# Two weight blocks split ahead of the first sums, the rest behind them, in a two-layer decoder trunk on one core

## The chip, the core and the metric

The kernel runs on one core of one Trainium2 chip. The metric is the device time of one execution in microseconds. The engines are named as in the profile: PE (matrix multiply), DVE (vector), ACT (scalar), POOL (GpSimd) and SP (which issues most loads from memory).

## The reference

The reference is a trunk of two layers with fp32 inputs. A layer is a half-step SwiGLU, a token mixer, and another half-step SwiGLU; a final RMS norm follows. With 256 tokens, width 1024 and 2816 hidden columns, the part that matters here is

```
def swiglu(x, w_gate, w_up, w_down):
    return (jax.nn.silu(x @ w_gate) * (x @ w_up)) @ w_down

x = x + 0.5 * swiglu(rms_norm(x, norm_ffn1[l]), w_ffn1_gate[l], w_ffn1_up[l], w_ffn1_down[l])
x = x + hybrid_mixer(rms_norm(x, norm_mix[l]), w_in[l], ...)
x = x + 0.5 * swiglu(rms_norm(x, norm_ffn2[l]), w_ffn2_gate[l], w_ffn2_up[l], w_ffn2_down[l])
```

So there are six phases in a row: SwiGLU, mixer, SwiGLU, SwiGLU, mixer, SwiGLU. The kernel numbers them `pi` 0 to 5.

## The kernel before

**Precision.** Every fp32 weight block of 128x1024 is split into a high part `whi` (ACT casts the raw block `wraw`, L260) and a low part `wlo` (DVE subtracts, L290). The same is done to the activations (`xh`, `xl`, side by side in `x2`). A product is made of three terms: high by high, high by low, low by high.

**Stream.** One `Stream` object carries all weight blocks in the order of their use. `loads` issues the transfers on SP into 5 buffers `wraw`. `split` issues the ACT cast of the next block and then the DVE subtraction of the block before it, which it had kept in `waiting`; `low` issues a subtraction that is still kept. The subtraction frees the block's `wraw` buffer, and the next load follows. There are 7 pairs of buffers for `whi` and `wlo`; `done` gives a pair back when PE has used it. `split` stops when none is free.

**SwiGLU phase.** The 2816 hidden columns are 22 groups of 128, numbered `j`. Group `j` needs a gate block and an up block; below they are called G0, U0, G1, U1, G2, and so on, and D0, D1 are the blocks of the down projection. `wide` multiplies one block in 8 steps; each step is a matmul of 512 columns with `whi` (L594) and one of 256 columns with `wlo` (L596). The two results of an even group go into two PSUM banks called psB, those of an odd group into psC and psD; each of these banks is single, so a group needs the banks of the group two before it to be read out. `read(j)` does that: per block ACT copies one half of the bank into the tile `hs` (L680) and DVE adds the other half to it (L681). These are the sums that the change speaks of. `finish(j)` then scales (POOL L691), applies SiLU (ACT L692), scales again (POOL L693), multiplies gate by up (DVE L695) and splits the product into `hp` (ACT L696, DVE L698), which the down matmuls (L572 to L574) take in.

**Start of a phase.** In the phases with `pi` > 0 the first two groups are multiplied by `gu_two`: first one half of the inner dimension for all four blocks, then `late()` turns the second half of the activations (`x_turn`, ACT L388 and DVE L389), then the second half of the inner dimension for all four. Then come `read(0)`, `read(1)` and the next round with the groups 2 and 3.

**What sets the order.** The program is written as one sequence; a scheduler with a timing model of its own then fixes the order of instructions on each engine, and on the chip every engine takes its instructions in that order. The kernel steers it with `st.behind`: what `split` and `low` put on ACT or DVE is queued behind the instruction named there (`queue`, L226). `x_turn` sets both entries to its last parts; `read(0)` sets the DVE entry to its last sum (L683). The phases 2, 3 and 5 are those with `gu_two` and `read` in this form; the mixers set `behind` by themselves.

Of the kernel before, what the change touches and what calls it, by code (L numbers as in the profile page):

```python
# [29 lines left out]
D, S, L, DH = 1024, 256, 2, 64  # L30
# [51 lines left out]
def all_units(phases):  # L82
    return [u for ph, l in phases for u in phase_units(ph, l)]
# [234 lines left out]
def trunk(ctx, tc, xin, wst, w1st, gains, glast, cst, small, out, phases=PHASES, n_raw=5, n_hl=7):  # L318
    nc = tc.nc
    V, A, G, T = nc.vector, nc.scalar, nc.gpsimd, nc.tensor  # L320
# [7 lines left out]
    st = Stream(nc, wst, all_units(phases), rawp, hlp, n_raw, n_hl)  # L328
# [3 lines left out]
    def load_aside(dst, src):  # L332

        with tc.issue_after(st.last):
            nc.sync.dma_start(dst, src)
# [3 lines left out]
    def bank(tag):  # L339
        return ps.tile([128, 512], F32, name="ps" + tag, tag="ps" + tag, bufs=BUFS[tag])  # L340
# [54 lines left out]
    def half_of(h):  # L395
        return slice(h * 512, (h + 1) * 512)
# [192 lines left out]
    def wide(o, u, ks):  # L589

        hi, lo = u[1]
        for k in ks:
            x = state["x2"][:, k]
            T.matmul(o, blk128(hi, k), x.rearrange("p a t -> p (a t)"), start=k == 0, stop=k == KT - 1,  # L594
                     skip_group_check=True)
            last = T.matmul(o[:, S:], blk128(lo, k), x[:, 0], start=False, stop=k == KT - 1,  # L596
                            skip_group_check=True).ins
        return last

    def wide_apart(o, u):  # L600

        hi, lo = u[1]
        for k in range(KT):
            T.matmul(o, blk128(hi, k), state["x2"][:, k].rearrange("p a t -> p (a t)"), start=k == 0, stop=k == KT - 1,
                     skip_group_check=True)
        for k in range(KT):
            T.matmul(o[:, S:], blk128(lo, k), state["x2"][:, k, 0], start=False, stop=k == KT - 1,
                     skip_group_check=True)

    def first_pair(os, us):  # L610

        xh, xl = state["xh"], state["xl"]
        for i, (o, u) in enumerate(zip(os, us)):
            hi, lo = u[1]
            for n in range(KT + 2 * LAG):
                if i == 0 and 0 < n < KT:
                    with tc.issue_after(real):
                        T.matmul(idle[:, :256], zero[:, :128], zero, start=True, stop=True)
                for p, (w, x, c) in enumerate(((hi, xh, 0), (hi, xl, S), (lo, xh, S))):
                    k = n - p * LAG  # L620
                    if 0 <= k < KT:
                        real = T.matmul(o[:, c:c + S], blk128(w, k), x[:, k], start=p == k == 0,
                                        stop=p != 1 and k == KT - 1, skip_group_check=True).ins
            st.done(u[0])
# [19 lines left out]
    def ffn(pi, name, l):  # L644
        nxt = pi + 1
        gu_tags = ["BB", "CD"]
        pend, S_ = {}, {}
        H = {}

        def gu_open(j):  # L650
            b = pend[j] = [bank(t) for t in gu_tags[j % 2]]
            return b, [st.use(what, name, l, j) for what in ("gate", "up")]

        def gu(j, mid=None):
            b, us = gu_open(j)
            if j == 0 and pi == 0:
                first_pair(b, us)
                return
            for o, u in zip(b, us):
                if j == 1 and pi == 0:  # L660
                    wide_apart(o, u)
                else:
                    wide(o, u, range(KT))
                st.done(u[0])
                if mid:
                    mid = mid()

        def gu_two():

            work = []  # L670
            for j in range(2):
                b, us = gu_open(j)
                work += [(lambda ks, o=o, u=u: wide(o, u, ks), [u]) for o, u in zip(b, us)]
            two_halves(work)

        def read(j):

            s = S_[j] = mp.tile([128, 2, S], F32, name="hs", tag="PT", bufs=5)
            for i, o in enumerate(pend.pop(j)):
                A.copy(s[:, i], o[:, S:])  # L680
                add = V.tensor_add(s[:, i], s[:, i], o[:, :S]).ins  # L681
            if j == 0 and pi > 0:
                st.behind["V"] = add  # L683

        def finish(j):
            n = 0 if j == NJ - 1 else 1
            s = S_.pop(j)
            g, u = s[:, 0], s[:, 1]
            hp = mp.tile([128, 2, S], F32R, name="hp", tag="qs", bufs=6)
            hh, hl = hp[:, 0], hp[:, 1]  # L690
            G.tensor_mul(g, g, state["rbc"])  # L691
            A.activation(g, g, AF.Silu)  # L692
            G.tensor_mul(g, g, state["rbc5"])  # L693
            st.split(n)
            V.tensor_mul(g, g, u)  # L695
            A.copy(hh, g)  # L696
            st.split(n)
            V.tensor_sub(hl, g, hh.bitcast(F32))  # L698
            st.split(3 - 2 * n)
            H[j] = hp  # L700

        def evac(j):
            read(j)
            finish(j)

        acc = {}
        last = nxt == len(phases)

        def down(j, u, t, h):
            if j == 0:  # L710
                acc[t, h] = bank("A")
            hi, lo = u[1]
            across(acc[t, h], t, H[j], hi[:, half_of(h)], lo[:, half_of(h)], j == 0, j == NJ - 1)

        def down_all(j):
            u = st.use("down", name, l, j)
            for h in range(2):
                for t in range(2):
                    down(j, u, t, h)
            st.done(u[0])  # L720
            del H[j]

        def down_tail():

            js = range(NJ - TAIL, NJ)
            us = {j: st.use("down", name, l, j) for j in js}
            if last:
                for t in range(2):
                    for n, (a, b) in enumerate(LAST[t]):
                        h, c = divmod(a, 512)  # L730
                        o = acc[t, h][:, c:c + b - a]
                        for j in js:
                            hi, lo = us[j][1]
                            across(o, t, H[j], hi[:, a:b], lo[:, a:b], False, j == NJ - 1)
                        last_add(t, n, o)
                    last_norm(t)
            else:
                for h in range(2):
                    turned = None
                    for j in js:  # L740
                        if h == 1 and j == NJ - TAIL // 2:
                            turned = x_turn(nxt, 0)
                        with tc.issue_after(turned) if turned else nullcontext():
                            for t in range(2):
                                down(j, us[j], t, h)
                    x_add(h, acc)

                def late():
                    x_turn(nxt, 1)
                    x_norm()  # L750
                state["late"] = late
            for j in js:
                st.done(us[j][0])
                del H[j]

        for p in range(NJ // 2):
            if p == 0:
                if pi == 0:
                    gu(0)
                    x_start_squares()  # L760
                    st.split(1)
                    gu(1, mid=norm_start)
                else:
                    gu_two()
                read(0)
                read(1)
                st.split(2)
                continue
            if p == 1:
                gu(2, mid=lambda: norm_bcast(True))  # L770
                finish(0)
                finish(1)
            else:
                gu(2 * p)
            evac(2 * p)
            gu(2 * p + 1)
            evac(2 * p + 1)
            for j in (2 * p - 2, 2 * p - 1) if p < NJ // 2 - 2 else ():
                down_all(j)
            if pi == 0 and p == 2:  # L780
                load_aside(cs_t[:, 128:], cst[:, 128:])
                load_aside(sm_t, small[:, :SMALL_COLS])
                load_aside(X.rearrange("p t d -> p (t d)"), small[:, SMALL_COLS:])
            if last:
                if p == 4:
                    load_gain()
            elif phases[nxt][0] == "mix" and p >= 5 and p < 9:
                load_w1(l, p - 5)
            st.split(1)
        for j in (NJ - TAIL - 2, NJ - TAIL - 1):  # L790
            down_all(j)
        down_tail()
# [615 lines left out]
```

## Time and profile before

| | |
|---|---|
| median of 3 runs | 1012.45 us (1012.07 to 1012.5) |
| profiled execution, its own time | 1012.55 us |
| its span, first to last instruction | 1010.5 us |
| PE busy | 995.4 us (99%) |
| DVE busy | 695.9 us (69%) |
| ACT busy | 592.3 us (59%) |
| POOL busy | 311.4 us (31%) |

The profiled execution is one run with every instruction recorded. Its time is 2.05 us more than the span of its instructions. Busy times say how full an engine is over the whole span; what a stall costs is read from the stretch in which it lies. On PE one matmul starts before the one before it has ended, so two starts that follow each other tell more than the duration of one.

### The profile page before, as it was taken

Reading aid. Unit: us, or ns where it says so; the run is one execution under the profiler, and the core shown is the slowest. Engines: PE = TensorE matmul, PEld = TensorE weight load, DVE = VectorE, ACT = ScalarE, POOL = GpSimd, SP = SyncE. Lnnn points to the kernel's source line nnn. Section 1 sums busy time; section 2 is a strip of 40 time slices with the busy share of each in tenths; the row PEclk is TensorE's granted clock in tenths of the full one; section 3 lists DMA queues with packets and bytes.
Section 4 is the critical chain, followed back from the end, with each engine's and each line's share of the span. In section 5 each row is a group of like instructions: output and inputs, shape, how many; then the busy total and the mean of one; then the engine's idle time right before and its main releaser. Section 6 shows DMA issues by size and latency. Waiting matters only on the chain.

```text
span 1010.5 us, 16093 instructions
## 1 busy us (share of the span) xinstructions
PE 995.4 (99%) x5873; PEld 861.1 (85%) x5873; DVE 695.9 (69%) x1163; ACT 592.3 (59%) x1137; POOL 311.4 (31%) x382
## 2 busy tenths in 40 slices
PE   9999999999999999999999999999999999999997
PEld 8888888899878888888888888889997788888885
DVE  7876666589974876666668666666898649665664
ACT  6755455558874655545565555456578756555552
POOL 2322132135741322213132222131476313222220
PEclk9999999999999999999999999999999999999999
DMA  8785766355542676666537677763546418766631
GB/s 277 251 296 192 272 245 217 101 178 154 168 152 63 211 231 192 191 195 190 159 130 256 189 234 233 279 188 119 163 117 188 139 34 275 220 207 192 189 122 42
DMA packets 52847, 188.20 MB, mean 186 GB/s; under 512 B 6368, under 2 KB 6752, under 8 KB 51616
## 3 DMA queue, kind: packets, MB, share of 16 engines
q1 hardware_dynamic: 49680, 182.17, 56.2%
q10 hardware_dynamic: 3088, 5.01, 1.9%
q8 instruction: 46, 0.75, 0.3%
q14 instruction: 33, 0.27, 0.1%
HBM read 182.04 MB, written 1.05 MB: 181 GB/s over the span
## 4 chain that ended last, share of the span: by engine, by line
PE 94%; DVE 3%; ACT 2%; issue 1%
PE psB L594 15%; PE psA L572 9%; PE psA L574 9%; PE psA L573 9%; PE psB L596 8%; PE psC L594 7%; PE psD L594 7%; PE psC L596 4%; PE psD L596 4%; PE psA L567 3%; PE psA L565 3%; PE psA L566 3%; ACT whi L260 1%; PE psD L1089 1%; PE psA L1079 1%; PE psA L1186 1%
## 5 line engine op out<-in xcount | busy, mean ns | idle before, releaser
L290 DVE TENSOR_TENSOR wlo<-wraw,whi 128x1024 fp32r<-128x1024 f32 x325 | 412.6, 1278 | 191.8 <-ACT whi L260 191.7
L260 ACT CAST whi<-wraw 128x1024 fp32r<-128x1024 f32 (+1 forms) x326 | 337.4, 1044 | 277.9 <-issue 157.0
L594 PE MATMUL psB<-x,whi 128*128 128x512 f32 x688 | 243.2, 393 | 1.3 <-DVE hs L681 1.3
L691 POOL TENSOR_TENSOR hs<-hs,rbc 128x256 f32<-128x256 f32 x88 | 76.7, 873 | 399.1 <-DVE hs L681 399.1
L596 PE MATMUL psB<-x,wlo 128*128 128x256 f32 x688 | 192.5, 280 | 1.9 <-DVE wlo L290 1.9
L594 PEld LDWEIGHTS psB<-x,whi 128*128 128x128 f32 x688 | 129.2, 188 | 30.2 <-DVE hs L681 2.2
L574 PE MATMUL psA<-wlo,hp 128*128 128x512 f32 (+1 forms) x356 | 137.6, 387 | 0.0
L573 PE MATMUL psA<-whi,hp 128*128 128x512 f32 (+1 forms) x356 | 137.5, 387 | 0.0
L572 PE MATMUL psA<-whi,hp 128*128 128x512 f32 (+1 forms) x356 | 134.1, 388 | 0.5 <-DVE X L470 0.5
L596 PEld LDWEIGHTS psB<-x,wlo 128*128 128x128 f32 x688 | 129.4, 188 | 4.6 <-DVE wlo L290 2.8
L693 POOL TENSOR_TENSOR hs<-hs,rbc 128x256 f32<-128x256 f32 x88 | 103.1, 1174 | 75.8 <-ACT hs L692 75.8
L594 PE MATMUL psC<-x,whi 128*128 128x512 f32 x344 | 122.0, 392 | 0.0
L594 PE MATMUL psD<-x,whi 128*128 128x512 f32 x344 | 121.7, 391 | 0.0
L596 PE MATMUL psC<-x,wlo 128*128 128x256 f32 x344 | 96.2, 280 | 0.0
L596 PE MATMUL psD<-x,wlo 128*128 128x256 f32 x344 | 96.2, 280 | 0.0
L572 PEld LDWEIGHTS psA<-whi,hp 128*128 128x128 f32 x356 | 66.6, 188 | 14.2 <-DVE X L470 0.7
L574 PEld LDWEIGHTS psA<-wlo,hp 128*128 128x128 f32 x356 | 66.8, 188 | 13.7
L573 PEld LDWEIGHTS psA<-whi,hp 128*128 128x128 f32 x356 | 66.9, 188 | 12.2
L594 PEld LDWEIGHTS psD<-x,whi 128*128 128x128 f32 x344 | 64.6, 188 | 14.3
L594 PEld LDWEIGHTS psC<-x,whi 128*128 128x128 f32 x344 | 64.6, 188 | 14.2
L565 PE MATMUL psA<-x,whi 128*128 128x256 f32 x256 | 73.0, 285 | 0.0
L567 PE MATMUL psA<-x,wlo 128*128 128x256 f32 x256 | 72.3, 282 | 0.0
(245 smaller groups left out, 1576.5 us busy)
## 6 DMA issues: line engine op xcount, KB each, us to landing
wraw<-in_w SPq DMA_DIRECT2D x318, 512.0 KB, 4.1
W1a<-in_w SPq DMA_DIRECT2D x4, 1024.0 KB, 5.8
W1mixn<-in_w SPq DMA_DIRECT2D x2, 1024.0 KB, 6.4
W1late<-in_w SPq DMA_DIRECT2D x2, 1024.0 KB, 6.0
KM<-KM ACTq DMA_DIRECT2D x8, 256.0 KB, 4.1
wraw<-in_w SPq DMA_DIRECT2D x4, 420.0 KB, 3.0
wraw<-in_w SPq DMA_DIRECT2D x4, 256.0 KB, 4.4
X<-in_small SPq DMA_DIRECT2D x1, 1024.0 KB, 6.8
```

Of the source, the lines that this page charges most:

```text
L260: self.last_hi = self.nc.scalar.copy(hi[:, a:b], raw[:, a:b]).ins
L290: eng.tensor_sub(lo[:, :c], raw[:, :c], hi[:, :c].bitcast(F32))
L565: T.matmul(o, hi, xh, start=first, stop=False, skip_group_check=True)
L566: T.matmul(o, hi, xl, start=False, stop=False, skip_group_check=True)
L567: return T.matmul(o, lo, xh, start=False, stop=last, skip_group_check=True).ins
L572: T.matmul(o, parts[:, 0, c], hi, start=first, stop=False, skip_group_check=True)
L573: T.matmul(o, parts[:, 1, c], hi, start=False, stop=False, skip_group_check=True)
L574: return T.matmul(o, parts[:, 0, c], lo, start=False, stop=last, skip_group_check=True).ins
L594: T.matmul(o, blk128(hi, k), x.rearrange("p a t -> p (a t)"), start=k == 0, stop=k == KT - 1, skip_group_check=True)
L596: last = T.matmul(o[:, S:], blk128(lo, k), x[:, 0], start=False, stop=k == KT - 1, skip_group_check=True).ins
L691: G.tensor_mul(g, g, state["rbc"])
L693: G.tensor_mul(g, g, state["rbc5"])
```

## The change

`read(0)` and `read(1)` now both set both entries of `st.behind`: splits that come later are queued on ACT behind the last copy and on DVE behind the last sum of the read. Ahead of `read(0)`, and so still behind the parts of `x_turn` alone, two blocks (G2 and U2, the third gate and up blocks of the phase) are split, and `low` issues the subtraction of the second one at once.

```
             for i, o in enumerate(pend.pop(j)):
-                A.copy(s[:, i], o[:, S:])
+                copy = A.copy(s[:, i], o[:, S:]).ins
                 add = V.tensor_add(s[:, i], s[:, i], o[:, :S]).ins
-            if j == 0 and pi > 0:
-                st.behind["V"] = add
+            if j < 2 and pi > 0:
+                st.behind["A"], st.behind["V"] = copy, add
...
                 else:
                     gu_two()
+
+                    st.split(2)
+                    st.low()
                 read(0)
                 read(1)
                 st.split(2)
```

Both programs hold the same numbers of instructions on PE, DVE and ACT; SP's list is the same. The orders differ only at the starts of the phases 2, 3 and 5, in three stretches. The line numbers in the rows below are the same in both files, since the new lines stand further down.

DVE at the start of phase 2, before (x: the last parts of `x_turn`; hs: the sums; wlo: the low parts):

```order
L389 SCALAR_TENSOR_TENSOR x_3529<-psA,g,x_3529 128x256 x4
L681 TENSOR_TENSOR hs<-hs,psB 128x256 x2
L290 TENSOR_TENSOR wlo<-wraw,whi 128x1024 x3
L681 TENSOR_TENSOR hs<-hs,psC 128x256
L290 TENSOR_TENSOR wlo<-wraw,whi 128x1024 x2
L681 TENSOR_TENSOR hs<-hs,psD 128x256
L695 TENSOR_TENSOR hs<-hs 128x256
```

The same place on DVE now:

```order
L389 SCALAR_TENSOR_TENSOR x_3529<-psA,g,x_3529 128x256 x4
L290 TENSOR_TENSOR wlo<-wraw,whi 128x1024 x2
L681 TENSOR_TENSOR hs<-hs,psB 128x256 x2
L681 TENSOR_TENSOR hs<-hs,psC 128x256
L681 TENSOR_TENSOR hs<-hs,psD 128x256
L290 TENSOR_TENSOR wlo<-wraw,whi 128x1024
L695 TENSOR_TENSOR hs<-hs 128x256
L290 TENSOR_TENSOR wlo<-wraw,whi 128x1024 x3
L695 TENSOR_TENSOR hs<-hs 128x256
L290 TENSOR_TENSOR wlo<-wraw,whi 128x1024
L681 TENSOR_TENSOR hs<-hs,psB 128x256
L698 TENSOR_TENSOR hp<-hs,hp 128x256
```

Two subtractions, those of G2 and U2, moved ahead of the four sums; the subtractions of G3, U3 and later moved behind all four.

ACT at the same place, before (whi: the casts; rbc: two copies for the norm; the table load belongs to the first SiLU of the phase):

```order
L388 ACTIVATE x_3529<-psA,g 128x256 x4
L260 CAST whi<-wraw 128x1024 x3
L550 COPY rbc<-psA 128x256
L554 ACTIVATE rbc_3715<-psA 128x256
L260 CAST whi<-wraw 128x1024
L680 COPY hs<-psB 128x256
L260 CAST whi<-wraw 128x1024
L680 COPY hs<-psB 128x256
L680 COPY hs<-psC 128x256
L680 COPY hs<-psD 128x256
L692 ACT_TABLE_LOAD
L692 ACTIVATE hs<-hs 128x256
```

The same place on ACT now:

```order
L388 ACTIVATE x_3529<-psA,g 128x256 x4
L260 CAST whi<-wraw 128x1024 x2
L550 COPY rbc<-psA 128x256
L554 ACTIVATE rbc_3724<-psA 128x256
L680 COPY hs<-psB 128x256 x2
L680 COPY hs<-psC 128x256
L692 ACT_TABLE_LOAD
L692 ACTIVATE hs<-hs 128x256
L680 COPY hs<-psD 128x256
L260 CAST whi<-wraw 128x1024 x4
L692 ACTIVATE hs<-hs 128x256
L260 CAST whi<-wraw 128x1024
```

Three of the five casts that stood among the copies moved behind the copy of psD, and that copy moved behind the table load and the first SiLU. Phase 5 has the same order; phase 3 has no table load there.

## Rows read from the trace of the kernel before

**Rows 1.** The page, part 1: busy us, share, instructions of each engine.
```profile
PE 995.4 (99%) x5873; PEld 861.1 (85%) x5873; DVE 695.9 (69%) x1163; ACT 592.3 (59%) x1137; POOL 311.4 (31%) x382
```

**Rows 2.** Stretches: length, then busy us (instructions) of each engine; clock, DMA share.
```profile
core 0: us, PE busy (x) PEld busy (x) DVE busy (x) ACT busy (x) POOL busy (x), PEclk, DMA share, GB/s
331.66:344.60 12.94, 11.66 (x67) 9.77 (x65) 12.37 (x15) 8.53 (x16) 5.97 (x5) 1.00 0.67 231
344.60:512.00 167.40, 167.40 (x892) 144.28 (x891) 108.33 (x151) 88.86 (x152) 41.95 (x53) 1.00 0.62 190
...
517.82:530.07 12.25, 11.61 (x66) 9.76 (x65) 12.25 (x15) 6.36 (x13) 5.52 (x4) 1.00 0.71 241
...
829.80:842.74 12.94, 11.65 (x66) 9.76 (x65) 12.36 (x15) 8.63 (x16) 6.03 (x5) 1.00 0.66 234
```

**Rows 3.** Waits of PE, whole span: total us, times, longest.
```profile
PE psB L596 <- DVE wlo L290: 1.9, 3, 0.6
...
PE psB L594 <- DVE hs L681: 1.3, 2, 0.7
```

**Rows 4.** Timeline of PE, phase 2: start, us, instruction, idle before and releaser.
```profile
328.42 0.28 PE L596 MATMUL psB<-x,wlo 128*128 128x256 f32 x1
...
331.54 0.28 PE L596 MATMUL psD<-x,wlo 128*128 128x256 f32 x1
331.66 0.40 PE L594 MATMUL psB<-x,whi 128*128 128x512 f32 x1
332.71 0.51 PE L594 MATMUL psB<-x,whi 128*128 128x512 f32 x1 [0.65 <-DVE hs L681]
333.84 0.39 PE L596 MATMUL psB<-x,wlo 128*128 128x256 f32 x1 [0.63 <-DVE wlo L290]
...
339.05 0.39 PE L594 MATMUL psC<-x,whi 128*128 128x512 f32 x1
...
344.60 1.07 PE L572 MATMUL psA<-whi,hp 128*128 128x512 f32 x4
345.51 0.40 PE L594 MATMUL psB<-x,whi 128*128 128x512 f32 x1
```

**Rows 5.** Timeline of ACT, the same stretch.
```profile
326.29 2.93 ACT L260 CAST whi<-wraw 128x1024 fp32r<-128x1024 f32 x3
329.12 0.37 ACT L550 COPY rbc<-psA 128x256 f32<-128x256 f32 x1
...
330.59 0.39 ACT L680 COPY hs<-psB 128x256 f32<-128x256 f32 x1
...
331.81 0.39 ACT L680 COPY hs<-psB 128x256 f32<-128x256 f32 x1
...
332.76 1.28 ACT L692 ACT_TABLE_LOAD   x1
334.06 0.42 ACT L692 ACTIVATE hs<-hs 128x256 f32<-128x256 f32 x1
337.52 1.06 ACT L260 CAST whi<-wraw 128x1024 fp32r<-128x1024 f32 x1 [3.05 <-DMA wraw<-in_w]
```

**Rows 6.** Timeline of DVE, the same stretch.
```profile
331.01 0.42 DVE L681 TENSOR_TENSOR hs<-hs,psB 128x256 f32<-128x256 f32 x1 [4.11 <-ACT hs L680]
332.23 0.42 DVE L681 TENSOR_TENSOR hs<-hs,psB 128x256 f32<-128x256 f32 x1 [0.80 <-ACT hs L680]
332.57 4.03 DVE L290 TENSOR_TENSOR wlo<-wraw,whi 128x1024 fp32r<-128x1024 f32 x3
...
340.00 0.63 DVE L695 TENSOR_TENSOR hs<-hs 128x256 f32<-128x256 f32 x1
...
345.51 0.95 DVE L698 TENSOR_TENSOR hp<-hs,hp 128x256 fp32r<-128x256 f32 x1
```

**Rows 7.** Timeline of POOL, the same stretch.
```profile
331.51 0.73 POOL L691 TENSOR_TENSOR hs<-hs,rbc 128x256 f32<-128x256 f32 x1 [6.42 <-DVE hs L681]
334.55 0.97 POOL L693 TENSOR_TENSOR hs<-hs,rbc 128x256 f32<-128x256 f32 x1 [2.31 <-ACT hs L692]
```

**Rows 8.** Waits of ACT, whole span: total us, times, longest.
```profile
ACT whi L260 <- DMA wraw<-in_w: 22.8, 20, 4.1
```

## The prediction

> **What bounds the kernel now.** I read the page's busy times first. PE is busy for 995.4 of 1010.5 us and no other engine reaches 70% [rows 1], so the time is PE's own work plus the places where PE stands still, and only a change that touches those places can show. Next came PE's waits over the whole span. Two lines belong to the starts of the phases 2, 3 and 5: three waits for `wlo`, 1.9 us together, and two for the sums `hs`, 1.3 us [rows 3]. Then I opened the timeline at the first of these places. After the last step of `gu_two` at 331.54 PE starts one step of G2 at 331.66, and then stands: the next start is at 332.71, released by the second sum of psB, and the one behind it at 333.84, released by the `wlo` of G2 [rows 4]. After that nothing holds PE: from 344.60 to 512.00 it is busy for 167.40 of 167.40 us [rows 2].
>
> Why it stands is read from the other two engines. DVE had nothing to do for 4.11 us up to 331.01 [rows 6], that is from 326.90. In this time ACT had already made three casts, from 326.29 on [rows 5], so subtractions were ready to be done, but they stood behind the sums of psB in DVE's order. The sums waited for ACT's copies, which came at 330.59 and 331.81 with casts between them [rows 5]. So the second sum ended at 332.65, and the first subtraction came only behind it [rows 6].
>
> **What the stall costs.** The idle time that the waits name is too small a measure, since PE also refills after each. I take the stretch instead. G2, U2, G3 and U3 are 32 steps. Unhindered, the last 16 of them run from 339.05 to 344.60, 5.55 us or 0.347 a step [rows 4], so 32 steps need 11.10 us. The stretches took 12.94, 12.25 and 12.94 us [rows 2]. Lost: 1.84 + 1.15 + 1.84 = 4.83 us. This is what there is to win here.
>
> **The change part by part.** No instruction is added or removed on PE, DVE or ACT, and SP keeps its order; everything is a matter of when. I walk through phase 2 with the new order, on the old time axis up to PE's 331.66.
>
> *Two casts and two subtractions first.* A cast takes about 0.98 us (three in 2.93), a subtraction 1.34 (three in 4.03, the slow ones of the stretch). ACT casts G2 and U2 from 326.29 to 328.2. DVE subtracts G2 until 328.6 and U2 until 329.95, in the time in which it was idle. PE wants G2's low part at 331.9 and U2's three microseconds later. Covered by idle DVE time; if that cover were gone, the cost is in the third rival.
>
> *The sums of psB.* ACT makes the two rbc copies behind the second cast instead of the third, until about 328.8. G0's last step ends at 328.70 [rows 4], so the copy runs 328.8 to 329.2, and the sum behind the second subtraction, 329.95 to 330.4. PE needs that bank at 331.66: 1.3 us to spare. U0's bank is complete three steps later (1.04 us), its sum done by 330.8; PE needs it only at 331.66 + 8 x 0.347 = 334.4. Both waits go.
>
> *The added wait: G3 and all behind it.* Casts now stand behind the copy of psD, and this behind the table load and the first SiLU. G1's bank is complete at about 330.8, its copy done at 331.2; table load 1.28 until 332.5; SiLU 0.42 until 332.9 (POOL's 0.73 for it runs from 330.4 [rows 7], so it is no bound); copy of psD until 333.3; cast of G3 until 334.3; subtraction until 335.6. PE wants G3 at 331.66 + 16 x 0.347 = 337.2: 1.6 us to spare. U3 stands behind the multiply L695 (0.63 [rows 6]; its input comes from POOL at about 332.9 + 0.97 = 333.9 [rows 7]) and is done at 337.6 against 340.0. What this wait can cost: nothing, as walked; at the other end, one load wait of ACT such as the 3.05 us before the cast at 337.52 [rows 5], which would put G3 at 338.65 and cost 1.44 us at each of the three starts. I take nothing, because five casts in a row ran before without such a wait (326.29 to 331.9, of which the fourth and fifth are the blocks U3 and D0), so G3, U3 and D0 lie in `wraw` already, and because the two early subtractions free two buffers about 5 us sooner. SP's list is unchanged, so the loads of D1 and G4 follow then; from the end of the old first subtraction (333.9) to the cast of the block loaded for it (337.52) passed 3.6 us, so D1 lies there by 332.2 and G4 by 333.6, both before ACT comes to them at 336.
>
> *What comes behind.* DVE then holds the low parts of D0 and D1 (until 340.3), a multiply (340.9), G4's low part (342.2), a sum (342.7), and L698, 0.95 us, which finishes `hp` of group 0 at 343.6 [rows 6]. PE reaches D0 at 331.66 + 11.10 = 342.76, and the matmuls that need that second half of `hp` only after four of D0 (0.91, from 344.60 to 345.51 [rows 4]) and two steps of G4: at 344.4. That is 0.8 us to spare with slow subtractions throughout. So this is the tightest place of the walk.
>
> A rule of the Trainium skill speaks against this part. ACT's table load took 1.28 us here, and the SiLU started 0.02 us behind its end [rows 5]. The skill's page "ScalarE: Activation LUTs", section "What ACT_TABLE_LOAD costs", gives nearly the same for the load but adds a drain, 2.66 us in all for each switch. By the page everything behind the load comes 1.38 us later: G3 would still arrive 0.2 us early, but L698 0.6 us too late, in the phases 2 and 5; the sum would be 4.83 - 1.2 = 3.6 us. By the row it stays 4.83. I go by the row.
>
> *Given back later?* From 344.60 on DVE has 108.33 us of work in 167.40 and ACT 88.86 [rows 2], so PE, 1.84 us ahead, still sets the pace to the next phase. Phase 3 has no table load and more to spare; phase 5 is phase 2 again.
>
> **Sum.** 1012.55 - 4.83 = 1007.72 for an execution like the profiled one. That execution was 0.10 us above the median of the runs, so 1007.6 against 1012.45.
>
> **Rivals.**
> First: part of the stall comes back, at G3, at D0 or at L698. For it: the spare times of 0.8 to 1.6 us are small beside single waits of ACT for loads of up to 4.1 us, of which there are 20 in the span [rows 8]. Against it: the blocks in question are loaded early. With 0.6 to 1.2 us lost at each start the gain is 1.2 to 3.0 us, so 1009.4 to 1011.2.
> Second: no change. The wait for G3 takes the whole place of the removed one, 1.44 us by the load wait above plus a refill (two waits of 1.28 us in all cost 1.84 before, so 0.28 for one): 1.72 at each start. That is 0.12 less than before at the phases 2 and 5 and 0.57 more at phase 3: 1012.45 + 0.33, about 1012.8. Against it: nothing in the old trace shows these three blocks late.
> Third, slower: the sums now stand behind the subtractions on DVE, and the copies behind the casts on ACT, so a late block U2 holds both banks of psB. The sum of G0's bank is planned to end at 330.4, PE's need is 331.66, and the old loss is 1.84: it turns to a loss when U2 is more than 3.1 us late. With ACT's longest wait for a load, 4.1 us [rows 8], it is 1.0 us worse at the phases 2 and 5 and 1.7 at phase 3, in all 3.7: 1016.1. Against it: ACT's third cast followed the second without a wait [rows 5], so U2 was there by 327.3.
>
> **How the numbers follow.** Forecast (all three stalls go, give or take 0.3 us each) 0.82; first rival 0.10; second 0.05; third 0.03. The likeliest gives 1007.6, its own range 1007.1 to 1008.5. With most of the first rival the range is 1007.0 to 1009.8. Below, there is little: the waits at the start of these phases are all counted, so only scatter (0.4 us between the runs) is left. What can be told from no change is 0.2%, about 2 us. The forecast and two thirds of the first rival lie beyond it: faster 0.89; the rest of the first rival and most of the second: same 0.07; the third and a bit of the second: slower 0.04.
>
> **What would show it.** In the changed profile DVE's subtractions of G2 and U2 stand at about 327.3 to 330, before the sums; the sum of the first psB ends before PE's first step of G2; PE has no wait for `hs` L681 or `wlo` L290 at psB, and from the last step of `gu_two` to D0's first matmul 11.1 us pass in all three phases. The walk is wrong if PE waits at psC for `wlo`, or at L573 for `hp`; the whole idea is wrong if those 11.1 us appear and the time does not fall, since then something later sets the pace.

## The result, and the profile after

The changed kernel takes 1007.62 us (median of 4 runs, 1006.79 to 1007.98), the kernel before 1012.32 on the same chip (4 runs). The ratio is 0.9948, 95% interval 0.9937 to 0.996, so 4 to 6.4 us are gained. The forecast was 1007.6. The profiled execution took 1007.35 us with a span of 1005.5, against 1012.55 and 1010.5 before.

First PE, the engine that sets the time. These are all of its waits that the view names over the span (total us, times, longest). The two lines of [rows 3], on psB, are gone.

```profile
PE psA L1189 <- DVE rotmq L828: 1.8, 2, 0.9
PE psA L1082 <- POOL P L1075: 1.4, 4, 0.6
PE psA L355 <- DVE zero L352: 1.1, 1, 1.1
PE psA L572 <- DVE X L470: 0.5, 1, 0.5
```

Nothing waits for the sums L681 or for `wlo` at psB any more. The three stretches of 32 steps, in the columns of [rows 2]:

```profile
331.80:342.90 11.10, 11.10 (x66) 9.76 (x65) 9.02 (x12) 9.56 (x15) 3.55 (x4) 1.00 0.62 209
516.18:527.28 11.10, 11.10 (x66) 9.76 (x65) 10.39 (x13) 9.24 (x14) 2.49 (x3) 1.00 0.68 237
826.66:837.77 11.11, 11.11 (x66) 9.77 (x65) 9.03 (x12) 9.68 (x15) 3.55 (x4) 1.00 0.62 218
```

PE's busy time equals the length of each. Against 12.94, 12.25 and 12.94 that is 1.84 + 1.15 + 1.83 = 4.82 us, nearly all of the 5.0 us by which the span fell. On PE's timeline of phase 2 [rows 4] the steps now follow each other:

```profile
331.68 0.28 PE L596 MATMUL psD<-x,wlo 128*128 128x256 f32 x1
331.80 0.39 PE L594 MATMUL psB<-x,whi 128*128 128x512 f32 x1
332.03 0.28 PE L596 MATMUL psB<-x,wlo 128*128 128x256 f32 x1
...
342.90 1.07 PE L572 MATMUL psA<-whi,hp 128*128 128x512 f32 x4
...
344.51 0.39 PE L573 MATMUL psA<-whi,hp 128*128 128x512 f32 x1
```

DVE at the same place [rows 6]. The two early subtractions stand in time in which it had nothing to do, and both sums of psB are done at 330.74. The first of them takes 0.41 us and so ends at about 330.2, 1.6 us ahead of PE's first step of G2 at 331.80, which needs only this bank. U2's first step, which needs the other, comes eight steps later, at about 334.6.

```profile
327.49 2.36 DVE L290 TENSOR_TENSOR wlo<-wraw,whi 128x1024 fp32r<-128x1024 f32 x2 [0.45 <-ACT whi L260]
329.77 0.97 DVE L681 TENSOR_TENSOR hs<-hs,psB 128x256 f32<-128x256 f32 x2
...
334.30 1.23 DVE L290 TENSOR_TENSOR wlo<-wraw,whi 128x1024 fp32r<-128x1024 f32 x1 [0.53 <-ACT whi L260]
...
335.78 4.04 DVE L290 TENSOR_TENSOR wlo<-wraw,whi 128x1024 fp32r<-128x1024 f32 x3
...
341.54 0.41 DVE L698 TENSOR_TENSOR hp<-hs,hp 128x256 fp32r<-128x256 f32 x1
```

And ACT [rows 5]:

```profile
326.42 1.99 ACT L260 CAST whi<-wraw 128x1024 fp32r<-128x1024 f32 x2
...
330.96 0.37 ACT L680 COPY hs<-psC 128x256 f32<-128x256 f32 x1 [0.67 <-PE psC L596]
331.35 1.28 ACT L692 ACT_TABLE_LOAD   x1
332.64 0.42 ACT L692 ACTIVATE hs<-hs 128x256 f32<-128x256 f32 x1
332.96 0.35 ACT L680 COPY hs<-psD 128x256 f32<-128x256 f32 x1
333.22 3.90 ACT L260 CAST whi<-wraw 128x1024 fp32r<-128x1024 f32 x4
```

The four casts behind the copy of psD run in one piece: G3, U3, D0 and D1 lay in their buffers when ACT came to them. Over the whole span ACT's waits for loads fell from 22.8 us [rows 8] to

```profile
ACT whi L260 <- DMA wraw<-in_w: 12.3, 12, 2.0
```

### The profile page after: what moved, and what is told of

The parts are those of the page before. It is cut to its first block, busy times and chain, and to the rows that moved or that the text cites. A ratio compares the mean times of both kernels' runs of the same rounds, so it can differ in the third digit from the quotient of the medians.

```text
span 1005.5 us, 16106 instructions
## 1 busy us (share of the span) xinstructions
PE 993.9 (99%) x5873; PEld 861.4 (86%) x5873; DVE 688.8 (68%) x1163; ACT 592.6 (59%) x1137; POOL 308.6 (31%) x382
## 4 chain that ended last, share of the span: by engine, by line
PE 96%; ACT 2%; DVE 1%; ACTq 0%; issue 0%
PE psB L594 16%; PE psA L572 9%; PE psA L574 9%; PE psA L573 9%; PE psB L596 8%; PE psC L594 8%; PE psD L594 8%; PE psD L596 4%; PE psC L596 4%; PE psA L567 3%; PE psA L565 3%; PE psA L566 3%; PE psD L1092 1%; PE psA L407 1%; PE psA L1189 1%; PE psA L1190 1%
## 5 line engine op out<-in xcount | busy, mean ns | idle before, releaser
L290 DVE TENSOR_TENSOR wlo<-wraw,whi 128x1024 fp32r<-128x1024 f32 x325 | 407.6, 1264 | 196.0 <-ACT whi L260 195.7
L691 POOL TENSOR_TENSOR hs<-hs,rbc 128x256 f32<-128x256 f32 x88 | 74.8, 852 | 386.6 <-DVE hs L681 368.2
L573 PE MATMUL psA<-whi,hp 128*128 128x512 f32 (+1 forms) x356 | 137.6, 387 | 0.0
L693 POOL TENSOR_TENSOR hs<-hs,rbc 128x256 f32<-128x256 f32 x88 | 101.9, 1159 | 86.5 <-ACT hs L692 86.5
L573 PEld LDWEIGHTS psA<-whi,hp 128*128 128x128 f32 x356 | 66.9, 188 | 12.3
```

What stands on the lines that cost most here:

```text
L290: eng.tensor_sub(lo[:, :c], raw[:, :c], hi[:, :c].bitcast(F32))
L573: T.matmul(o, parts[:, 1, c], hi, start=False, stop=False, skip_group_check=True)
```

## The experiments

Each ratio is to the kernel before, run on the same chip. Where a diff is against the kernel before, this is said; the others are against the changed kernel. The changed kernel itself, run once more beside the second set of experiments, gave 1008.13 us (ratio 0.9951, 0.9939 to 0.9963).

> The changed kernel once more, beside the kernels of this call, for a comparison on the same chip and at the same time. Both theories: 0.5% under the kernel before, about 4.8 us.

### The early split alone

Against the kernel before:

```
                 else:
                     gu_two()
+
+                    st.split(2)
+                    st.low()
                 read(0)
```

> Only the early split of G2 and U2 is made; the entries of behind stay as in the kernel before. Theory (PE stood because the first subtractions stood behind the sums of psB in DVE's order; the early split alone puts them ahead): ACT still has casts among the copies, so the sums of psB end at about 331.4 and 332.6 as before, but G2 and U2 are ready by 330, and the bank of U2 is wanted only at 334.4. All of 4.8 us goes: 1007.6 us, give or take 0.6. Rival (the gain needs the casts out from between ACT's copies, so that the sums come sooner): the second wait stays, 0.8 us or more at two of the starts, and G3's sums of psC, behind three subtractions again, come late: 1009.5 to 1012.

Measured: 1007.84 us, ratio 0.9952 (0.994 to 0.9965), and no wait of PE at psB. DVE in phase 2:

```profile
327.37 2.36 DVE L290 TENSOR_TENSOR wlo<-wraw,whi 128x1024 fp32r<-128x1024 f32 x2 [0.45 <-ACT whi L260]
331.03 0.42 DVE L681 TENSOR_TENSOR hs<-hs,psB 128x256 f32<-128x256 f32 x1 [1.30 <-ACT hs L680]
332.25 0.42 DVE L681 TENSOR_TENSOR hs<-hs,psB 128x256 f32<-128x256 f32 x1 [0.80 <-ACT hs L680]
```

The second sum stands where it stood before (332.25 against 332.23 in [rows 6]), and yet PE does not wait for it. PE's order in the kernel before tells why (numbers of the buffers kept; psB_3689 is G2's bank, psB_3690 U2's):

```
L594 MATMUL psB_3689<-x2_3529,whi_3680 128x512
L594 MATMUL psB_3690<-x2_3529,whi_3683 128x512
L596 MATMUL psB_3689<-x2_3529,wlo_3681 128x256
```

The matmul that waited for the second sum was U2's first one, which the scheduler had put ahead of G2's first low part. It stands so at all three starts. With the early split U2's matmuls follow behind all of G2's, 2.8 us later, when the second bank has long been read. So one cause, the late low part of G2, made both waits: with that low part early, the wait for the second sum went too, although the sum came no sooner. The whole gain is that of the early splits; the queueing half adds nothing that can be measured. (Why the scheduler chose the old order is not shown; the order itself is.)

### The queueing half alone

Against the kernel before, the new `read` without the two early splits:

```
-                A.copy(s[:, i], o[:, S:])
+                copy = A.copy(s[:, i], o[:, S:]).ins
...
-            if j == 0 and pi > 0:
-                st.behind["V"] = add
+            if j < 2 and pi > 0:
+                st.behind["A"], st.behind["V"] = copy, add
```

> Only the queueing is made: all splits after the reads stand behind the copies and sums, and there is no early split. Theory: the copies come early and the banks of psB are free in time, but the cast of G2 starts only behind the copy of psD and the table load, at about 332.5, its low part is ready at 334.7; PE stands about 3.0 us at the phases 2 and 5 and 2.7 at phase 3, against 1.84 and 1.15 before: 1016.4 us (1015 to 1018). Rival (the queueing carries the gain by bringing the sums sooner): 1008 to 1010.

Measured: 1019.17 us, ratio 1.006 (1.0046 to 1.0074): slower as expected, by more than expected. PE's first wait line is

```profile
PE psB L594 <- ACT whi L260: 5.9, 6, 1.6
```

and PE's timeline of phase 2 shows two things, a stand and what comes after it:

```profile
331.59 0.28 PE L596 MATMUL psD<-x,wlo 128*128 128x256 f32 x1
333.46 0.51 PE L594 MATMUL psB<-x,whi 128*128 128x512 f32 x1 [1.59 <-ACT whi L260]
334.41 0.50 PE L594 MATMUL psB<-x,whi 128*128 128x512 f32 x1 [0.44 <-ACT whi L260]
335.26 0.38 PE L596 MATMUL psB<-x,wlo 128*128 128x256 f32 x1 [0.34 <-DVE wlo L290]
...
336.73 0.63 PE L594 MATMUL psB<-x,whi 128*128 128x512 f32 x1
```

ACT comes to its five casts only behind the copy of psD, at 332.35, so G2 is late from its cast on. A matmul that took 0.39 us takes up to 0.63 in the stretch from 336.18 on. The granted clock is the third figure from the right in these rows, a stretch from each of the three phases:

```profile
336.18:339.71 3.53, 3.53 (x13) 2.96 (x12) 3.53 (x4) 2.53 (x5) 1.30 (x1) 0.52 0.91 317
...
524.00:528.00 4.00, 4.00 (x16) 3.42 (x15) 4.00 (x4) 3.44 (x6) 0.76 (x1) 0.57 0.80 237
838.50:841.25 2.75, 2.70 (x9) 2.02 (x8) 2.75 (x4) 2.75 (x5) 0.00 (x0) 0.50 0.48 133
```

About 0.5 is the lower of the clock's two levels, 1.2 GHz. Before, the stalls that cost 1.84 us left it at 1.00 [rows 2].

### The queueing half with PE kept busy

The kernel of the last experiment, with 24 matmuls on zeros behind `gu_two` (additional work; their result is read by nothing) and the norm's broadcast moved ahead of them:

```
-                    last = f(ks)
+                    last = state["gu_last"] = f(ks)
...
                     gu_two()
+                    norm_bcast(True)
+                    fill = bank("A")
+                    with tc.issue_after(state["gu_last"]):
+                        for _ in range(24):
+                            T.matmul(fill[:, :256], zero[:, :128], zero, start=True, stop=True)
...
-                gu(2, mid=lambda: norm_bcast(True))
+                gu(2, mid=(lambda: norm_bcast(True)) if pi == 0 else None)
```

> As the kernel with the queueing alone (1019.2 us, 1018.25 to 1020.25), but PE does 24 matmuls on zeros of 256 columns behind the last step of gu_two while it waits for G2; their result is not used. In the trace of the queueing alone PE stood about 3 us at each start, and the granted clock in the 3 to 4 us behind was 0.50 to 0.62. Theory (2.8 us of its time, by which it missed its expectation, is the clock that fell after the wait): with PE kept busy the clock stays at 1.00, the waits for G2 stay as they are, and the time is 1016.4 us (1015 to 1017.5). Rival (the excess is a longer wait, not the clock): no change or more, 1019 to 1021.

Measured: 1017.12 us, ratio 1.0045 (1.0031 to 1.0059). The filler, on PE's timeline:

```profile
332.14 2.79 PE L769 MATMUL psA<-zero 128*128 128x256 bf16 x24
```

The stretches behind it, in the columns of [rows 2]:

```profile
335.20:340.00 4.80, 4.51 (x26) 3.81 (x26) 4.80 (x5) 3.65 (x6) 1.31 (x1) 1.00 0.60 191
523.60:528.00 4.40, 4.40 (x28) 3.86 (x27) 4.40 (x5) 3.22 (x6) 0.77 (x1) 1.00 0.79 275
839.00:842.00 3.00, 3.00 (x19) 2.67 (x18) 3.00 (x3) 0.87 (x4) 1.30 (x1) 1.00 0.93 314
```

The clock stays at 1.00, so it was the stand that took it down. What this is worth is read from the last step of `gu_two` to the first matmul of D0, the same matmuls in both kernels beside the filler. At phase 2, first the queueing alone, then with the filler:

```profile
331.59:347.57 15.98, 13.60 (x66) 11.11 (x65) 15.22 (x18) 12.94 (x20) 5.61 (x5) 0.89 0.67 231
332.02:346.44 14.42, 14.13 (x91) 12.12 (x90) 13.61 (x17) 11.37 (x18) 4.41 (x4) 1.00 0.63 221
```

G2's first low part comes 3.67 us behind that last step in both (335.26 and 335.69), so the wait itself is unchanged. The three starts took 15.98, 15.27 and 15.55 us and now take 14.42, 13.87 and 14.42: 4.1 us less. That fits the 3.53 x 0.48 + 4.00 x 0.43 + 2.75 x 0.50 = 4.8 us of clock that the slowed stretches had lost. The whole time shows less of it: 3.0 us by the spans, 2.05 by the medians of runs on two chips, 0.0015 or 1.5 us by the ratios, whose intervals overlap. The profiled execution of the queueing alone was the longest of its four, 1020.25 us.

### One block early, and three

The figure in the early split set to 1, and to 3:

```
-                    st.split(2)
+                    st.split(1)
```

> As the changed kernel, but only G2 is split early; U2 stands with the rest behind the copies. Theory, by the same walk: U2's cast runs at 332.5 to 333.4 and its low part is ready at 334.6, just when PE comes to its first low part at 334.66; nothing or up to 0.3 us is lost at two starts: 1007.6 to 1008.3 us. Rival (both blocks have to be early, since the waits were for both banks of psB): about half of the gain, 1009.5 to 1010.5.

Measured: 1008.96 us, ratio 0.9959 (0.9947 to 0.9972). One small wait at U2's low part appears on PE's timeline:

```profile
335.24 0.38 PE L596 MATMUL psB<-x,wlo 128*128 128x256 f32 x1 [0.17 <-DVE wlo L290]
```

The same wait stands at phase 5. From the last step of `gu_two` to D0 the three starts take 11.65, 11.22 and 11.67 us, against 11.21 each with the early split of both blocks alone: U2's early split is worth 0.9 us and G2's the rest of the 4.8. The time is above the theory's range and below the rival's; the theory had the place right and its price, up to 0.3 us at each of two starts, somewhat low (0.45).

```
-                    st.split(2)
+                    st.split(3)
```

> As the changed kernel, but three blocks (G2, U2, G3) are split ahead of the first sums. Theory (in-order walk): three casts end at 329.2, three subtractions at about 330.95, the first sum of psB at 331.3 against a need at 331.66: still in time, by some 0.3 us, and G3 gets more room; 1007.6 us, or up to 0.5 more where the sum is just late. Rival (two early blocks are all that the idle DVE time holds, the third one delays the sums): 0.5 to 1.2 us lost at each start, 1009.2 to 1011.

Measured: 1007.53 us, ratio 0.9944 (0.9929 to 0.9958), not to be told from the changed kernel. DVE:

```profile
328.05 3.50 DVE L290 TENSOR_TENSOR wlo<-wraw,whi 128x1024 fp32r<-128x1024 f32 x3 [0.45 <-ACT whi L260]
331.46 0.75 DVE L681 TENSOR_TENSOR hs<-hs,psB 128x256 f32<-128x256 f32 x2
```

In this execution PE comes to its first step of G2 at 332.35, all else being later too. Three subtractions fill most of the idle time: both sums are done at 332.21, the first at about 331.9, half a microsecond ahead. A fourth of 1.17 us would by this estimate push the first sum past the need; it was not run.

### The sums made late

U2's subtraction is done four times, and the sums of psB stand behind all four (the additional three leave the same values):

```
-                eng.tensor_sub(lo[:, :c], raw[:, :c], hi[:, :c].bitcast(F32))
+                for _ in range(times):
+                    self.last_low = eng.tensor_sub(lo[:, :c], raw[:, :c], hi[:, :c].bitcast(F32)).ins
...
+                with tc.issue_after(st.last_low) if j == 0 and pi > 0 else nullcontext():
+                    add = V.tensor_add(s[:, i], s[:, i], o[:, :S]).ins
...
-                    st.low()
+                    st.low(4)
```

> As the changed kernel, but U2's subtraction is done four times over (the same values), and the sums of psB stand behind all of them on DVE. It tests the in-order walk and the third rival of the prediction: sums that are held up behind subtractions. Theory: five subtractions of 1.17 us and two sums put the first sum of psB at about 334.7 on the changed kernel's time axis where PE wants it at 331.8; PE stands 2.9 us there, with refill 3.1 at the phases 2 and 5, and about 2.0 at phase 3: 1007.6 + 8.2 = 1015.8 us (1014.5 to 1017). Rival (PE is not bound by these banks, or the starts have several microseconds to spare): under 1010.

Measured: 1016.48 us, ratio 1.0044 (1.0026 to 1.0061). This is DVE's part of the third rival, made to happen. DVE's sums of psB (lines are shifted by two in this kernel):

```profile
334.82 0.74 DVE L683 TENSOR_TENSOR hs<-hs,psB 128x256 f32<-128x256 f32 x2
```

On PE the scheduler put a first step of G3 and, at the phases 2 and 5, of U3 ahead of G2, so most of the wait bears the name of their casts. The last row is G2's first step at phase 5:

```profile
331.99 0.28 PE L597 MATMUL psD<-x,wlo 128*128 128x256 f32 x1
333.68 0.49 PE L595 MATMUL psC<-x,whi 128*128 128x512 f32 x1 [1.41 <-ACT whi L260]
334.62 0.80 PE L595 MATMUL psD<-x,whi 128*128 128x512 f32 x1 [0.45 <-ACT whi L260]
335.29 0.79 PE L595 MATMUL psB<-x,whi 128*128 128x512 f32 x1
...
835.64 0.50 PE L595 MATMUL psB<-x,whi 128*128 128x512 f32 x1 [0.17 <-DVE hs L683]
```

PE had but two matmuls between 331.99 and 335.29; behind that the granted clock averages 0.89 from 336 to 345, so a part of the price is again the clock. The rival's mechanism exists: at the phases 2 and 5 G2's first step started when the first sum was done, about 3.1 us late. Its price is not shown by the agreement with 1016.1. The sums were late by 3.1, 1.7 and 3.1 us where the rival reckoned 2.84 at each start, the casts of G3 and U3 held PE for most of that time, and the clock added to it. In the changed kernel the first sum is 1.6 us early, so the rival does not act.

### The same idea at the wait that is left

The largest line of waits left on PE is at L1189: 0.91 us in each of the two mixers. Its bank is read by the rotary multiply L828 of the memory queries (`rotmq`), and that multiply stood on DVE behind a weight subtraction and behind `P` L1053, the first softmax step of the first head. DVE in the changed kernel:

```profile
267.69 1.22 DVE L290 TENSOR_TENSOR wlo<-wraw,whi 128x1024 fp32r<-128x1024 f32 x1
268.89 0.48 DVE L1053 CUSTOM_DVE_ANT_0 P<-psB,const,nrs 128x256 f32<-128x256 f32 x1
...
269.30 0.68 DVE L828 TENSOR_TENSOR rotmq<-psA,const 128x512 f32<-128x512 f32 x1
```

First the subtraction alone was queued behind the multiply (`turned` is the instruction L828, returned by `rope_begin`):

```
-                rope_begin(cur["b"], raw, sw, ro, tabs[0])
+                turned = rope_begin(cur["b"], raw, sw, ro, tabs[0])
                 ends.append((which, h, sw, ro, tabs[1]))
+                if which == "mq" and h == 1:
+                    st.behind["V"] = turned
```

> The changed kernel, and in the two mixers one subtraction of a weight block is queued behind the multiply that empties the psA bank of the last moba query (rotmq), in place of ahead of it. PE waits 0.9 us for that multiply in each mixer, and before it on DVE stands a subtraction of 1.22 us. Theory (the same cause at another place: low parts that nobody wants yet stand ahead of an operation that frees a bank): both waits go with their refill, 2 x 1.1 us: 1005.4 us (1004.8 to 1006.2). Rival (another wait at that place takes over, for POOL's P or for the block that now comes later): 1007 to 1008.

Measured: 1007.4 us, ratio 0.995 (0.9938 to 0.9962): no difference, against expectation. PE's wait is the same 0.9 us, twice. DVE shows why:

```profile
268.88 0.48 DVE L1053 CUSTOM_DVE_ANT_0 P<-psB,const,nrs 128x256 f32<-128x256 f32 x1 [1.12 <-PE psA L1082]
...
269.29 0.69 DVE L828 TENSOR_TENSOR rotmq<-psA,const 128x512 f32<-128x512 f32 x1
```

Where the subtraction stood DVE now idles for 1.12 us: `P` now stands first and waits for PE (the trace names the transposes L1082, and the scores L1284 that `P` reads start behind them, at 268.48). The subtraction had lain in time that was lost anyway; what held the multiply was `P`. So in the next version the multiply goes ahead of `P` as well:

```
+                if which == "mq" and h == 1:
+                    st.behind["V"] = cur["turned"] = turned
...
-        moba_s(0)
+        with tc.issue_after(cur["turned"]):
+            moba_s(0)
```

> The changed kernel, with rotary's multiply put ahead of both the weight subtraction and the first softmax step of the first head on VectorE's stream, in both mixers. Theory: the multiply then has nothing in front of it that waits for TensorE; its bank is complete by 267.0 us, so it ends by 268.5 and TensorE's wait of 0.9 us at L1191 is gone in both mixers; with the refill that is about 1.1 us each, 2.2 in all: 1005.0 to 1005.8 us (ratio to the kernel before about 0.9929). Rival: the subtraction (1.2 us) now stands ahead of the first softmax step, which ends 1.2 us later, and TensorE waits for it instead, at the transposes of the first head: 1007 to 1008 us, with a wait at L1082 that is longer than the 0.6 us there now.

Measured: 1005.02 us (5 runs), ratio 0.9925 (0.9911 to 0.9938). The theory held. On DVE:

```profile
267.93 0.68 DVE L828 TENSOR_TENSOR rotmq<-psA,const 128x512 f32<-128x512 f32 x1
268.53 1.35 DVE L290 TENSOR_TENSOR wlo<-wraw,whi 128x1024 fp32r<-128x1024 f32 x1
269.80 0.47 DVE L1053 CUSTOM_DVE_ANT_0 P<-psB,const,nrs 128x256 f32<-128x256 f32 x1
```

and PE goes on without a wait (L1191 is L1189 of the changed kernel):

```profile
269.29 0.39 PE L1191 MATMUL psA<-whi,x 128*128 128x512 f32 x1
```

From the same transposes (265.90 and 266.13) to this matmul pass 3.16 us instead of 4.23, so 1.07 us come from the first mixer. `P` is 0.9 us later, and PE does not wait for it. The longest wait at L1082 did grow, to 0.89 us at 759.94 in the second mixer, but it stands ahead of the multiply, so it is not the rival's; the version before it has the same wait (0.89 us at 760.83), and its cause was not traced. The span is 1.9 us below that of the changed kernel. This version beats the kernel before. That it also beats the changed kernel is carried by the trace more than by the times: the two were not run side by side on one chip, and its interval (up to 0.9938) just touches the first one of the changed kernel (from 0.9937) and stays just below the second (from 0.9939).

## Why the prediction was right

**What bounds.** Only places where PE stands were counted, and the gain came from them: 4.82 of the 5.0 us of span. That the median, 1007.62 us, meets the forecast of 1007.6 so closely is partly luck: the four runs spread over 1.2 us.

**The size.** The step that made it right was taking the loss from the stretch and not from the waits' names. The named waits that went are 1.9 and 1.3 us [rows 3], 3.2 in all; the stretches gave back 4.82 against 4.83 forecast. The remaining 1.6 us, the refills of the forecast, stand under no wait: a wait counts from the end of the matmul before, while unhindered the next one starts 0.23 us after a matmul of 512 columns that is listed with 0.39 (331.80 to 332.03).

**Two casts and two subtractions first.** Right in mechanism, and shown alone to be the whole gain, four fifths of it G2's block. The subtractions took 1.18 us each, not 1.34, the price of the slow ones.

**The sums of psB.** Both were forecast to be done by 330.8 and were at 330.74. (The times of the forecast are on the old axis, on which PE comes to G2 at 331.66; now it comes at 331.80.) But the forecast gave the wait for the second sum a remedy of its own, copies with no casts between them. The experiment with the early split alone shows that it needed none: the wait was a consequence of G2's late low part in the scheduler's order.

**The added wait.** G3's low part was forecast for 335.6 and ended at 335.53; the load wait that could have cost 1.44 us at each start did not come, and ACT's waits for loads fell from 22.8 to 12.3 us in all.

**What comes behind.** L698 was forecast to end at 343.6 with 0.8 us to spare; it ended at 341.95, 2.56 us ahead of L573 at 344.51. I had charged 1.34 for every subtraction, 0.63 for the multiply and 0.95 for L698; one subtraction took 1.21, and the multiply and L698 0.41 each. So L698 was not the tightest place of the walk; of the places that the walk names, that was the first sum of psB, with 1.6 us (forecast 1.3).

**The table load.** The copy ahead of it ended at 331.33, the load ran from 331.35 to 332.63, and the SiLU started at 332.64: no drain stands on either side. The trace thus does not agree with the 2.66 us that the Trainium skill's page "ScalarE: Activation LUTs", section "What ACT_TABLE_LOAD costs", gives for a switch. These rows decide it, and the gain does not: the 3.6 us that the forecast worked out from that figure came from L698 being 0.6 us late by slow prices, and with the 2.56 us that L698 had to spare in fact, 1.38 us more would not have shown in the time.

**The rivals.** No part of the stall came back at G3, D0 or L698. The second rival would have needed a load wait that did not occur. The third was made to happen by the late sums, at 1016.48 us against 1016.1; its working left out that the clock fell in such a stand and reckoned other delays than those made, so the agreement in size is luck.

## What to carry to other kernels

When PE stops twice within a few matmuls, measure the whole stretch against its unhindered pace: here the named waits were two thirds of the loss. Where an engine with a fixed order idles ahead of a wait, put into that time the due work whose inputs are already there, and look first at what the engine really waits for: the early split paid because DVE idled for 4.11 us ahead of the first sum, while moving a subtraction out of the mixer paid nothing, since the next instruction there was waiting as well. Queueing work behind something without moving the urgent part ahead first can cost more than the stall that it was to cure.

## What was not expected of the hardware

At the three starts of the queueing alone PE did only two matmuls in 3.0 to 3.7 us (at phase 2 from 331.59 to 335.26). Around the end of that time its granted clock fell, to about 0.5, the 1.2 GHz level, in the stretches of 2.75 to 4.00 us shown above, and a 512-column matmul took 0.63 us instead of 0.39. The stalls that cost 1.84 us in the kernel before left it at 1.00. With matmuls on zeros in that time it stayed at 1.00. What happens between these cases no run shows.
